# A two-layer decoder trunk on one core: work of layer 1 that waits for room on the vector engine, a later start of the key stage, and a shorter step of the recurrence

## The chip, the core and the metric

The kernel runs on one core of a Trainium2 chip. A core has a matrix engine (TensorE, PE in the profile; its weight loads are PEld), a vector engine (VectorE, DVE), a scalar engine (ScalarE, ACT), a general one (GpSimd, POOL), and SyncE (SP), which here only issues transfers. The program fixes the order of the instructions on each engine (the helper `InOrder`). An instruction whose input is late therefore holds up what is listed behind it on that engine. The metric is the device time of one execution in microseconds (us). The runs of the kernel before took 2396.8, 2400.13 and 2401.81 us, so the median is 2400.13 us.

## What is computed

The input is x with 512 positions of 2048 features. Layer 0 is forgetting attention and layer 1 is RWKV-7 time mixing. Both sit between a modulated RMS norm and a gated residual addition. All of the change lies in layer 1, cut here to what matters:

```
xr, xw, xk, xv, xa, xg = h + (shifted h - h) * mu[i]
r, k, v, z = xr @ Wr, xk @ Wk, xv @ Wv, xg @ Wz          # 2048 x 2048 each
decay, a, mix of v:  low-rank products tanh(xw @ w1) @ w2, (xa @ a1) @ a2, (xv @ v1) @ v2
kk = normalised(k * k_k);  k = k * (1 + (a - 1) * k_a)
S = S * w + (S a) b + v k ;  y = S r                      # a scan over 512 positions, 32 heads
y = group_norm(y) * lnx_w + lnx_b + sum(r * k * r_k) * v  # the last term is the "bonus"
out = x + gate * ((y * silu(z)) @ Wo)
```

## The kernel before, in words

Every large product is computed from float32 operands that are split in two parts each, `hi` and `lo`. ACT writes the `hi` part (a copy with rounding), DVE or POOL subtracts to get the `lo` part, and PE runs three matmuls of 128 x 128 by 128 x 512 for each block of 128 features. Weights arrive in blocks of four such tiles (`raw`, three buffers), and ACT makes `whi` and DVE makes `wlo` from each.

Layer 1 is written as a *backbone* and *tasks*. The backbone is the list of all output tiles of Wk, Wr, Wv, Wz and Wo, 16 tiles for each matrix (some of Wk's are made earlier), each with 16 steps of three matmuls into a PSUM bank named `pj`. The tasks are Python generators. When one says `yield 3`, it is resumed three planner units later. The planner's clock `fl.t` is advanced by every matmul listed, by its columns over 2400, so three matmuls of 512 columns take 0.64 units. After each backbone step, `Flow.run` resumes all tasks that are due, and these list their own instructions. So the planner's clock decides the **order** on every engine, and nothing in it is a real wait on the chip. Real waits are the semaphores that the tiles bring with them.

The tasks are started by `side`, one stage after the other:

- `lora_k`, `lora_w`, `lora_up`: the low-rank products. Their last results go to DRAM (`aad`, `svd`, `ipd`).
- A `yield 3`, then the pools are changed, POOL clears some tiles, and `keys` begins: 16 tasks, one every `KEY` = 9.8 units. A key task loads `ip`, `kt`, `aa`, squares on ACT (`sq`), has the mean of the squares made on PE (helper `means`: ACT `mhi`, DVE `mlo`, two matmuls into bank `S`), and then runs a string of ACT and DVE operations. It stores `at`, `bk`, `gab`.
- `invert` and `inverse`: for each group of four keys, 30 steps of two elementwise operations that invert triangular blocks. Groups 0 to 2 use POOL, group 3 uses DVE (`lt`, `lane`). The results go through `qt`.
- When all of these are done: `stages` and `recur`. `stage` prepares two chunks of 64 positions for a group of eight heads (`rt`, `prk`, `L`, `SV`, `QP`), with 18 transfers of its own. `products` makes their small matrices, `bonus` makes `bv`, and `recur` walks 32 chunks of the recurrence. Each chunk has three dependent links on PE (`x<-SV,L`, `x<-xs,QP`, `x<-SV,tok`), with a DVE copy or sum between them. A link is listed when the planner's clock passes a multiple of `HOP` (3.9 units). `normed` normalises the output of two chunks (`dc`) and stores it to `ypd`.
- `gated` belongs to the backbone tiles of Wz. It takes the silu on ACT (`z`), waits until `ypd` is there, loads it (`yp`, one buffer), and multiplies on DVE. The product goes through `gd` into the activations of Wo.

`mixing` tasks reload the 16 activation tiles when the backbone changes from one matrix to the next. Such a change is a burst of 16 loads `hp`, 16 ACT `hi` and 16 `lo`.

Of the kernel before, what the change touches and what calls it, by code (L numbers as in the profile page):

```python
# [76 lines left out]
class InOrder:  # L77


    def __init__(self, tc, engine):  # L80
        self.tc, self.engine, self.on, self.last, self.clock = tc, engine, False, None, None

    def __getattr__(self, name):
        f = getattr(self.engine, name)

        def issue(*a, **k):
            with ExitStack() as s:
                if self.on and self.last is not None:
                    s.enter_context(self.tc.issue_after(self.last.ins))
                self.last = f(*a, **k)  # L90
            if self.clock and name in ("matmul", "transpose"):
                o, n = a[0], 1
                for d in o.shape[1:]:
                    n *= d
                w = o.shape[0] if a[1].shape[0] > 64 else o.shape[0] * a[1].shape[0] / P
                self.clock.t += (1 if a[2].dtype == R else 4) * n * w / P / 2400
            return self.last
        return issue

    @contextmanager  # L100
    def behind(self):
# [30 lines left out]
def body(ctx, tc, a, out, dbg=None, stop=0):  # L132
    nc = tc.nc
    pe, act, dve, pool, sp = (InOrder(tc, e) for e in (nc.tensor, nc.scalar, nc.vector,
                                                       nc.gpsimd, nc.sync))
# [260 lines left out]
    with ExitStack() as s0:  # L396
# [201 lines left out]
        fl = Flow()  # L598
# [325 lines left out]
        n = len(tiles)  # L924
# [112 lines left out]
    def col(v, j):  # L1037
        return vecs[:, v, j:j + 1]
# [4 lines left out]
    def u3(t):  # L1043
        return t.rearrange("p (u t) -> p u t", u=NU)
# [7 lines left out]
    fl = Flow()  # L1052
# [41 lines left out]
    def read(tag, n):  # L1094
        rings[tag][n] = fl.t + 0.7
# [14 lines left out]
    def take(tag):  # L1110
        while not free[tag]:
            yield 0.2
        free[tag] -= 1
# [363 lines left out]
    def stage(q, g, u):  # L1477

        rt = q.tile([P, NJ, UC, C], F, tag="rt", name="rt", bufs=2)
        sp.dma_start(rt.rearrange("p j c t -> p j (c t)"), rTd[g][:, u])  # L1480
        bk = q.tile([P, NJ, UC, 2, C], F, tag="bk", name="bk", bufs=2)
        yield 1
        for i in range(2):
            for h in range(2):
                sp.dma_start(bk.rearrange("p j c i t -> p (j c) i t")[HS[h], :, i, :],
                             bkd[g][HS[h], u, i ^ h].rearrange("p j (c t) -> p (j c) t", c=UC))
            yield 0.6
        yield from take("prk")
        prk = q.tile([P, NJ, UC, C], F, tag="prk", name="prk", bufs=2)
        sp.dma_start(prk.rearrange("p j c t -> p j (c t)"), ipd[g][:, u])  # L1490
        yield STW
        eI = q.tile([P, NJ, UC, C], F, tag="eI", name="eI", bufs=2)
        act.activation(eI, prk, AF.Exp, scale=-EDEC)
        yield 1
        dec = q.tile([P, NJ, UC], F, tag="dec", name="dec", bufs=3)
        pool.tensor_copy(dec, eI[:, :, :, C - 1])
        dve.tensor_tensor(out=rt, in0=rt, in1=eI, op=OP.mult)
        yield 1
        for j in range(NJ):
            for h in range(2):  # L1500
                s = HS[h]
                dve.scalar_tensor_tensor(out=prk[s, j], in0=rt[s, j],
                                         scalar=vecs[s, V_RK, NJ * g + j:NJ * g + j + 1],
                                         in1=bk[s, j, :, 1 - h, :], op0=OP.mult, op1=OP.mult)
            yield 0.6
        while any(NJ * g + i not in vd for i in range(NJ)):
            yield 0.2
        for c in range(UC):
            yield from take("chunk")
            m = NCH * g + UC * u + c  # L1510
            L, SV = ([q.tile([P, NJ] + w, F, tag=f"{m}{h}", name=f"{m}{h}", bufs=4)
                      for h in range(2)] for m, w in (("L", [2, C]), ("SV", [C])))
            svs[m] = SV
            qp = QP[m % 4]
            for h in range(2):
                s, t = HS[h], OS[h]
                sp.dma_start(L[h][s, :, 0, :], atd[g][s, u, :, c * C:c * C + C])
                dve.tensor_copy(L[h][s, :, 1, :], rt[s, :, c])
                sp.dma_start(qp[h][s], qtd[NJ * g:NJ * g + NJ, 64 * c:64 * c + 64,
                                           4 * h + u, :].rearrange("j p t -> p j t"))  # L1520
                sp.dma_start(SV[h][t], vtd[g][(UC * u + c) * C:(UC * u + c + 1) * C, h])
                if u == c == 0:
                    pool.memset(SV[h][s], 0.0)
                yield 0.6
            fl.start(fl.t + STW, products(q, m, c, L, SV, qp, bk, eI, dec))
            yield 2
        fl.start(fl.t + 2, bonus(q, g, u, prk))
# [41 lines left out]
    def bonus(q, g, u, prk):  # L1569
        vv = q.tile([P, T], F, tag="vv", name="vv", bufs=1)  # L1570
        sp.dma_start(vv.rearrange("p (j t) -> p j t", j=NJ), vvd[g][:, u])
        yield 6
        yield from take("B")
        bo, n = yield from means(q, blkr, prk.rearrange("p j c t -> p (j c t)"), "mh", "ml")
        free["B"] += 1
        yield 0.9
        yield from take("bv")
        bv = q.tile([P, T], F, tag="bv", name="bv", bufs=2)
        dve.scalar_tensor_tensor(out=bv, in0=bo, scalar=float(DH), in1=vv, op0=OP.mult,
                                 op1=OP.mult)  # L1580
        read("S", n)
        free["prk"] += 1
        staged[g, u] = bv

    def hop():
        n = fl.t // HOP
        while fl.t // HOP == n:
            yield 0.1
# [57 lines left out]
    def normed(q, g, u, y):  # L1646

        ys = q.tile([P, T], F, tag="ys", name="ys")
        act.activation(ys, y, AF.Copy)
        while (g, u) not in staged:  # L1650
            yield 0.2
        bv = staged.pop((g, u))
        yield 0.6
        yield from take("B")
        d, n = yield from means(q, centerr, ys, "mh", "ml")
        dc = q.tile([P, T], F, tag="ys", name="dc")
        sq = q.tile([P, T], F, tag="sq", name="sq", bufs=2)
        yield 0.7
        act.activation(sq, d, AF.Square)
        act.activation(dc, d, AF.Copy)  # L1660
        read("S", n)
        yield 1.5
        vr, n = yield from means(q, blkr, sq, "mh", "ml")
        free["B"] += 1
        yield 0.7
        if "silu" in tab:
            tab.clear()
            act.preload_act_table_set("natural_log_exp_and_others")
        r = rstd_of(q, vr, lneps, 64e-5, "sq", False, bufs=2)
        read("S", n)  # L1670
        yield 2
        for j in range(NJ):
            s = slice(j * P, (j + 1) * P)
            dve.scalar_tensor_tensor(out=dc[:, s], in0=dc[:, s], scalar=col(V_LW, NJ * g + j),
                                     in1=r[:, s], op0=OP.mult, op1=OP.mult)
        for j in range(NJ):
            s = slice(j * P, (j + 1) * P)
            dve.scalar_tensor_tensor(out=dc[:, s], in0=dc[:, s], scalar=col(V_LB, NJ * g + j),
                                     in1=bv[:, s], op0=OP.add, op1=OP.add)
        free["bv"] += 1  # L1680
        yield 1.8
        sp.dma_start(ypd[g][:, u], dc.rearrange("p (j t) -> p j t", j=NJ))
        if u == NU - 1:
            yd.update(range(NJ * g, NJ * g + NJ))
# [9 lines left out]
    def gated(j, o, e):  # L1694
        yield from until(e)
        yield from take("z")
        z = mq.tile([P, T], F, tag="z", name="z")
        act.activation(z, o, AF.Silu)
        freed.add(e)
        tab.add("silu")  # L1700
        while j not in yd:
            yield 0.2
        yp = mq.tile([P, T], F, tag="yp", name="yp", bufs=1)
        sp.dma_start(u3(yp), of(ypd, j))
        yield 4
        yield 1
        dve.tensor_tensor(out=z, in0=z, in1=yp, op=OP.mult)
        yield 1
        free["z"] += 1
        if j < KT - 2:  # L1710
            sp.dma_start(gd[j], z)
            zd.add(j)
        else:
            while len(G) < j:
                yield 0.2
            yield from halve(j, z)
# [35 lines left out]

    STW = 5
    DG, DINV = (3,), 32
    HOP = 3.9
    INV, KEY = 54, 9.8

    def side(q):
# [23 lines left out]
                yield 0.8  # L1782
        while len(ups) < 3 * KT:
            yield 0.2
        yield 3
        pools.close()
        kp = pools.enter_context(tc.tile_pool(name="kp", bufs=1, reuse_waits="tile"))
        eIs.append(kp.tile([P, NCH, C + 1], F, name="eI"))
# [40 lines left out]
    tiles += [(a["wo1"][j], G, output, j) for j in range(KT)]  # L1829
    for e in (pe, dve, act):  # L1830
        e.on = True
    pe.clock = fl
    freed.clear()
    n0, n1, n2, n3 = NK, NK + KT, NK + 2 * KT, NK + 3 * KT
    for n, task in ((n0, mixing(1, Ar, A)), (n1, mixing(0, Av, Ar)), (n2, mixing(2, Az, Av)),
# [25 lines left out]
```

## Time and profile before

| | |
|---|---|
| median of three runs | 2400.13 us (2396.8 to 2401.81) |
| profiled execution, its time | 2401.73 us |
| its span, first to last instruction | 2399.9 us |
| PE busy | 2302.2 us (96%) |
| DVE busy | 1605.2 us (67%) |
| ACT busy | 1256.5 us (52%) |
| POOL busy | 694.4 us (29%) |
| mean granted TensorE clock | 0.982 |

The page of the profile gives busy time by engine, then the span in 40 slices (busy tenths; PEclk is the granted TensorE clock in tenths), the chain that ended last, and groups of instructions with their mean time and with what ended the idle time before them. A line of the timeline reads: start, duration, engine, line, operation, output tile `<-` input tiles, sizes, count, and in brackets how long the engine had been idle and what ended that. `SPq` is a transfer being issued.

The first low-rank matmuls of layer 1 stand near 1191 us in the trace. The first loads of the key stage are issued at 1356 us, the recurrence's first links stand at 1738.6 us and its last at about 2172 us, and the product with Wo ends the kernel.

### The profile page before, as it was taken

To read this page: it belongs to the slowest core of one execution; us is meant where nothing else is said; L and a number is where in the kernel's file an instruction comes from. 1 tells how busy PE (TensorE), PEld (TensorE's weight loads), DVE (VectorE), ACT (ScalarE), POOL (GpSimd) and SP (SyncE) were. 2 spreads that over 40 slices of the span, in tenths; PEclk is the share of its full clock that TensorE was granted. 3 is DMA by queue.
4 is the path that set the end of the run, shared out by engine and by line. 5 is a ranking of instruction groups with operands and counts; after the bars stand their busy time and mean duration, and the time that the engine had idled before them with its cause. 6 is when DMAs were issued, how large, how long until landed. Compare 5 with 4: busy or idle time off the path is not lost. (4 is left out here: it accounts for less than half of the span.)

```text
span 2399.9 us, 39413 instructions
## 1 busy us (share of the span) xinstructions
PE 2302.2 (96%) x13626; PEld 1807.3 (75%) x13626; DVE 1605.2 (67%) x2850; ACT 1256.5 (52%) x2300; POOL 694.4 (29%) x1114
## 2 busy tenths in 40 slices
PE   6999999999999999998999898899999899999999
PEld 4787777877778778886777676677777677777787
DVE  6886778888888635336797567666476776755322
ACT  4435655555565545225646777763345556665221
POOL 0002333442424210110141208771245535450000
PEclk8999999999999999999999999899999999999999
DMA  8864466766666346445756999886867766544543
GB/s 307 328 227 156 128 211 217 222 213 213 205 224 220 114 161 225 142 141 157 223 179 198 308 263 277 256 252 187 233 187 195 219 174 194 167 132 154 161 137 97
DMA packets 388152, 480.23 MB, mean 200 GB/s; under 512 B 146032, under 2 KB 217840, under 8 KB 384112
## 3 DMA queue, kind: packets, MB, share of 16 engines
q1 hardware_dynamic: 386288, 475.08, 63.7%
q0 software_dynamic: 1664, 2.63, 0.3%
q8 instruction: 108, 1.77, 0.3%
q14 instruction: 92, 0.75, 0.1%
HBM read 381.63 MB, written 95.95 MB: 199 GB/s over the span
## 5 line engine op out<-in xcount | busy, mean ns | idle before, releaser
L90 PE MATMUL pj<-hi,whi 128*128 128x512 f32 x2416 | 987.4, 409 | 11.0 <-ACT hi L90 8.2
L90 PE MATMUL pj<-hi,wlo 128*128 128x512 f32 x2416 | 959.4, 397 | 10.1 <-DVE wlo L90 10.0
L90 PE MATMUL pj<-lo,whi 128*128 128x512 f32 x2416 | 959.9, 397 | 0.0
L90 DVE TENSOR_TENSOR wlo<-raw,whi 128x512 fp32r<-128x512 f32 (+2 forms) x628 | 473.4, 761 | 255.1 <-ACT whi L90 252.4
L90 ACT ACTIVATE whi<-raw 128x512 fp32r<-128x512 f32 (+2 forms) x628 | 393.9, 634 | 399.0 <-PE pj L90 215.1
L90 PEld LDWEIGHTS pj<-hi,whi 128*128 128x128 f32 x2416 | 459.5, 190 | 116.8 <-ACT hi L90 9.2
L90 PEld LDWEIGHTS pj<-lo,whi 128*128 128x128 f32 x2416 | 458.3, 190 | 108.4 <-DVE lo L90 0.7
L90 PEld LDWEIGHTS pj<-hi,wlo 128*128 128x128 f32 x2416 | 459.9, 190 | 105.2 <-DVE wlo L90 13.4
L90 DVE CUSTOM_DVE_ANT_0 wm<-wm,cb 128x1024 f32<-128x1024 f32 x128 | 155.8, 1217 | 0.3
L90 POOL TENSOR_SCALAR SV<-SV,dec 64x64 f32<-64x64 f32 x224 | 94.2, 442 | 103.9 <-DVE SV L90 69.7
L90 ACT ACTIVATE pr<-Sm,mx 128x128 f32<-128x128 f32 (+3 forms) x128 | 71.5, 559 | 76.8 <-POOL mx L90 76.3
L90 POOL TENSOR_SCALAR pr<-pr,rc 128x128 f32<-128x128 f32 (+3 forms) x128 | 100.8, 788 | 26.0 <-DVE rc L90 23.6
L90 POOL TENSOR_SCALAR mx<-mx 128x1 f32<-128x1 f32 x128 | 59.9, 468 | 143.2 <-DVE mx L90 98.0
L90 DVE CUSTOM_DVE_ANT_0 Sm<-S,cmask 128x128 f32<-128x128 f32 (+3 forms) x128 | 62.3, 487 | 42.5 <-PE S L90 41.8
L90 POOL TENSOR_TENSOR lt<-lane 128x30 f32<-128x30 f32 (+14 forms) x90 | 64.2, 713 | 86.4 <-DMA lane<-mld 79.6
L90 POOL TENSOR_TENSOR bk<-bk,eI 128x512 f32<-128x512 f32 x32 | 36.6, 1142 | 110.3 <-PE S L90 64.0
L90 POOL TENSOR_TENSOR lane<-lane,lt 128x30 f32<-128x30 f32 (+14 forms) x90 | 64.0, 711 | 7.0
L90 PE MATMUL S<-k,q 128*128 128x128 f32 (+7 forms) x256 | 61.9, 323 | 0.0
L90 POOL TENSOR_TENSOR acc<-acc,sq 128x512 f32<-128x512 f32 x14 | 18.1, 1296 | 149.4 <-ACT sq L90 128.2
L90 ACT ACTIVATE pT<-tr 128x512 f32<-128x512 f32 x64 | 31.0, 485 | 54.4 <-PE tr L90 54.4
L90 DVE SCALAR_TENSOR_TENSOR hp<-pj,gate,hp 128x512 f32<-128x512 f32 x16 | 12.0, 751 | 68.0 <-PE pj L90 68.0
L90 PE MATMUL tr<-ident,pr 128*128 128x128 f32 x320 | 56.0, 273 | 1.5 <-DVE pT L90 1.3
(325 smaller groups left out, 3284.0 us busy)
## 6 DMA issues: line engine op xcount, KB each, us to landing
wm<-in_wmodT SPq DMA_DIRECT2D x132, 512.0 KB, 4.4
raw<-in_wz SPq DMA_DIRECT2D x128, 256.0 KB, 3.7
raw<-in_wo SPq DMA_DIRECT2D x128, 256.0 KB, 3.6
raw<-in_wv SPq DMA_DIRECT2D x124, 256.0 KB, 3.9
wm<-in_wmodT SPq DMA_DIRECT2D x30, 1024.0 KB, 6.4
raw<-in_wk SPq DMA_DIRECT2D x96, 256.0 KB, 3.7
raw<-in_wr SPq DMA_DIRECT2D x64, 256.0 KB, 5.0
raw<-in_wq SPq DMA_DIRECT2D x56, 256.0 KB, 3.5
```

Source lines behind the costliest of these rows:

```text
L90: self.last = f(*a, **k)
```

## The change

There are three parts.

First, the helper around each engine gets an estimate of the time until which the engine is taken: `until`, advanced by 0.08 units plus 0.0008 for each column with every instruction listed on it. `dve.room()` makes a task wait, in the planner's clock, until DVE's estimate is no more than 0.6 units ahead. It is called in `stage`, `bonus`, `normed` and `gated`. SP gets the estimate too, but nothing asks for it. Second, the key stage begins 8 units behind the low-rank stage in place of 3. Third, `HOP` is 3.8 in place of 3.9.

```diff
@@ class InOrder
+        self.flow, self.until = None, 0
...
+            if self.flow and "table" not in name:
+                n = 1
+                for d in (k.get("out", a[0] if a else None)).shape[1:]:
+                    n *= d
+                self.until = max(self.until, self.flow.t) + (
+                    0.38 if name == "dma_start" else 0.08 + n * 8e-4)
+    def room(self, left=0.6):
+        while self.until - self.flow.t > left:
+            yield 0.2
@@ stage
+        yield from dve.room()
         dec = q.tile([P, NJ, UC], F, tag="dec", name="dec", bufs=3)
         pool.tensor_copy(dec, eI[:, :, :, C - 1])
         dve.tensor_tensor(out=rt, in0=rt, in1=eI, op=OP.mult)
         yield 1
         for j in range(NJ):
+            yield from dve.room()
             for h in range(2):
                 ...                                  # the two prk of this j
...
             for h in range(2):
                 s, t = HS[h], OS[h]
+                yield from dve.room()
                 sp.dma_start(L[h][s, :, 0, :], atd[g][s, u, :, c * C:c * C + C])
                 dve.tensor_copy(L[h][s, :, 1, :], rt[s, :, c])
@@ bonus
         yield from take("bv")
+        yield from dve.room()
         bv = q.tile([P, T], F, tag="bv", name="bv", bufs=2)
@@ normed
         for j in range(NJ):
+            yield from dve.room()
             ...                                      # dc times the weight and 1/deviation
         for j in range(NJ):
+            yield from dve.room()
             ...                                      # dc plus the bias and bv
@@ gated
-        yield 4
-        yield 1
+        yield 5
+        yield from dve.room()
         dve.tensor_tensor(out=z, in0=z, in1=yp, op=OP.mult)
@@
-    HOP = 3.9
+    HOP = 3.8
@@ side
         while len(ups) < 3 * KT:
             yield 0.2
-        yield 3
+        yield 8
         pools.close()
...
-    pe.clock = fl
+    pe.clock = dve.flow = sp.flow = fl
```

## The prediction

> **What bounds the kernel now.** I read the page first. PE is busy for nearly all of the span, so the time is PE's work plus what PE loses.
>
> ```profile
> span 2399.9 us, 39413 instructions
> PE 2302.2 (96%) x13626; PEld 1807.3 (75%) x13626; DVE 1605.2 (67%) x2850; ACT 1256.5 (52%) x2300; POOL 694.4 (29%) x1114
> PEclk8999999999999999999999999899999999999999
> ```
>
> The change adds and removes no instruction; it reorders them. PE's matmuls stay the same, so it can only move PE's idle time and the time at a lower clock. The second view cuts layer 1 into stretches (length, then busy time of PE, PEld, DVE, ACT, POOL, then granted clock, DMA share, GB/s).
>
> ```profile
> 1302.00:1376.00 74.00, 65.19 (x261) 49.78 (x262) 43.51 (x48) 57.93 (x97) 13.80 (x19) 0.96 0.95 303
> 1376.00:1600.00 224.00, 207.14 (x1412) 159.95 (x1411) 153.11 (x197) 161.07 (x299) 132.08 (x184) 0.94 0.91 262
> 1600.00:1640.00 40.00, 32.91 (x238) 25.12 (x237) 33.39 (x65) 17.44 (x33) 14.46 (x14) 0.87 0.70 219
> 1640.00:2186.00 546.00, 528.96 (x5140) 415.55 (x5141) 361.13 (x766) 293.75 (x516) 222.16 (x427) 0.99 0.66 184
> 2186.00:2240.00 54.00, 51.01 (x216) 39.88 (x215) 27.12 (x48) 26.68 (x44) 0.00 (x0) 1.00 0.60 188
> 2240.00:2400.00 160.00, 156.04 (x672) 126.19 (x670) 45.39 (x68) 33.41 (x53) 0.00 (x0) 1.00 0.42 128
> ```
>
> Length less PE busy is PE's idle time: 8.8 us up to the first key, 16.9 in the keys, 7.1 in the inversion of the last group, 17.0 in the recurrence, 3.0 at its end. The lower clock comes on top: 224 x 0.06 = 13 us in the keys and 40 x 0.13 = 5 in the inversion. So some 53 us of idle time and about 25 of clock lie where the change can reach. The third view is what ended PE's waits, in the inversion (first row), the recurrence (four) and its end (last); columns: total, times, longest.
>
> ```profile
> PE pj L90 <- DVE wlo L90: 7.1, 3, 2.8
> PE S L90 <- ACT GP L90: 9.7, 5, 5.3
> PE S L90 <- ACT mhi L90: 3.5, 1, 3.5
> PE S L90 <- DVE mlo L90: 1.8, 4, 0.6
> PE x L90 <- DVE SV L90: 1.2, 2, 0.9
> PE pj L90 <- DVE wlo L90: 2.9, 3, 1.5
> ```
>
> Last, the chain that ended last, at its end (start, duration, piece).
>
> ```profile
> 2199.92 4.51 DMA yp<-ypd
> 2204.45 0.70 DVE z L90
> ...
> 2226.59 169.46 PE pj L90 x728
> ```
>
> The recurrence's output passes through `yp` and `z` into Wo. PE meanwhile has other tiles and loses only the 2.9 us above. From 2226.59 it runs without a gap: 169.46 / 728 = 0.233 us for each matmul, for which the planner counts 512 / 2400 = 0.213 units. A planner unit is 1.09 us of chip time.
>
> **The change part by part.**
>
> *Keys from 3 to 8 units.* Everything behind this `yield` moves 5 x 1.09 = 5.5 us later against the backbone: POOL's clearing of the tiles, the key loads on SP, all key tasks, the inversions, the start of the recurrence. The place before:
>
> ```profile
> 1355.67 0.58 SPq L90 DMA_DIRECT2D ip<-ipd  x1
> 1365.23 0.63 ACT L90 ACTIVATE hi<-hp 128x512 fp32r<-128x512 f32 x1 [0.89 <-DMA hp<-mxd]
> 1368.94 0.61 ACT L90 ACTIVATE mhi<-sq 128x512 fp32r<-128x512 f32 x1
> 1369.67 0.68 DVE L90 TENSOR_TENSOR wlo<-raw,whi 128x512 fp32r<-128x512 f32 x1
> 1370.28 1.76 DVE L90 TENSOR_TENSOR mlo<-sq,mhi 128x512 fp32r<-128x512 f32 x1
> 1369.61 0.50 PE L90 MATMUL S<-mhi,blkr 128*128 128x512 f32 x1 [3.18 <-ACT mhi L90]
> 1372.09 0.79 PE L90 MATMUL S<-mlo,blkr 128*128 128x512 f32 x1 [1.99 <-DVE mlo L90]
> 1370.00:1375.00 5.00, 3.01 (x8) 2.33 (x8) 4.99 (x5) 4.85 (x9) 2.66 (x2) 0.50 0.96 253
> 1375.00:1380.00 5.00, 5.00 (x20) 4.00 (x19) 3.87 (x6) 3.71 (x8) 0.00 (x0) 0.82 0.97 349
> ```
>
> The first key's `mhi` and `mlo` stand on ACT and DVE among the `hi` and `lo` of the mixing burst that brings Wr's activations, whose loads `hp` are late. PE waits 3.18 + 1.99 = 5.2 us at the key's two matmuls. Then the clock is 0.50 for five us and 0.82 for five, a loss of 2.5 + 0.9 = 3.4, of which 1.0 falls into the 1.99 us idle already counted. Together that is 5.2 + 2.4 = 7.6 us. With the delay PE lists 5.5 us of backbone there, which covers the 5.2. Next late is the backbone's own `wlo`: PE came to the gap at 1369.61 - 3.18 = 1366.4, a block of weights lasts 12 x 0.233 = 2.8 us, so it wants the next at 1369.2, and the `wlo` above ended at 1370.35. I leave 1.5 us for this and its like: **-6** (ends: -7.6, and 0 if another wait takes its place). POOL's clearing and three more loads on SP then stand inside the burst; POOL was busy 13.8 of 74 us there, so I cost them at nothing. If that cover is gone, an odd `lo` is late and it comes out of the 6.
>
> *The other keys.* They move with the first, in the same order to one another: **0**. Ends: -5 (the 5.5 us of lead also shortens later waits), and +6 (rival 1).
>
> *The inversion of the last group* runs on DVE while the next mixing burst puts its `lo` and the `wlo` on the same queue:
>
> ```profile
> 1620.00:1640.00 20.00, 15.67 (x114) 11.90 (x113) 19.39 (x37) 7.06 (x13) 5.22 (x4) 0.82 0.59 163
> ```
>
> DVE is full, and the three waits for `wlo` (7.1 us) are here. The burst belongs to the backbone and stays; the inversion goes 5.5 us later, so 5.5 of some 35 us lie free of it. A share of 5.5 / 35 of 7.1 + 5 is 2; what follows the burst then gets the inversion's end, so I take half: **-1**. Ends: -6, and +5.5 if the end of it delays `wlo` as much as it moves.
>
> Whether short gaps cost clock matters here, since all three are under 3 us. Two stretches of the key stage show it:
>
> ```profile
> 1497.00:1500.00 3.00, 1.49 (x5) 1.00 (x6) 3.00 (x5) 1.63 (x4) 2.74 (x4) 0.95 1.03 322
> 1500.00:1503.00 3.00, 3.00 (x10) 1.89 (x8) 1.73 (x3) 2.19 (x4) 2.63 (x5) 0.50 1.03 316
> ```
>
> After 1.5 us of idle time in three, the next three ran at half clock. [...]
>
> *Hops of 3.8.* 32 chunks of three hops are 96 x 0.1 = 9.6 units, 10.5 us less. Against a start 5.5 us later the recurrence ends 5.0 us earlier beside the backbone. The first and last chunk, and who waits for whom on DVE:
>
> ```profile
> 1738.60 0.91 PE L90 MATMUL x<-SV,L 128*64 128x64 f32 x11
> ...
> 2172.42 0.69 PE L90 MATMUL x<-SV,L 128*64 128x64 f32 x16
> DVE SV L90 <- PE x L90: 47.2, 29, 3.7
> ```
>
> 31 chunks in 433.8 us are 14.0 us each, against 11.7 planned units x 1.09 = 12.8. DVE waits 47.2 us for PE at `SV`, and PE only 1.2 us, in two of 96 links, for DVE. So the links have air, and 0.11 us less in each is hidden there. Ends: +10.5 if each link were tight, +0.2 for the two; I take the latter. The earlier end gives at most the 2.9 us of the last stretch, since PE has no other gap behind the recurrence; as those `wlo` stand behind `z`, and `z` behind `yp`, whose one buffer and 4.5 us per load are unchanged, I take -0.2. Sum **0**, ends -3 and +10.5.
>
> *Room on DVE.* The estimate and the real durations (mean ns after the bar):
>
> ```profile
> L90 DVE TENSOR_TENSOR wlo<-raw,whi 128x512 fp32r<-128x512 f32 x135 | 97.1, 722 | 43.3 <-ACT whi L90 41.7
> L90 DVE SCALAR_TENSOR_TENSOR prk<-rt,vecs,bk 64x128 f32<-64x128 f32 x128 | 47.4, 371 | 1.7
> ```
>
> A 512-column operation counts 0.49 units, 0.53 us, and takes 0.72; a `prk` counts 0.18 units, 0.2 us, and takes 0.37. So DVE looks emptier than it is, and a task is held only where several operations are listed at one instant. Held are `rt`, `prk`, `L`, `bv`, `dc` and `z`; behind each are only its own task's steps, with `QP` and `SV` loads on SP behind the `L` copy, a PSUM bank of `S` behind `bv`, and `ypd` behind `dc`. Stages run up to four chunks ahead and cover a unit or two. In front of them go `wlo`, `mlo` and the links. DVE ended 2.9 + 1.8 + 1.2 = 5.9 us of PE's waits in the recurrence and its end; I take a quarter: **-1.5** (ends: -5.9, and +7, a further stall like the next). The larger waits, 9.7 and 3.5, come through ACT:
>
> ```profile
> 1911.91 0.89 SPq L90 DMA_DIRECT2D prk<-ipd  x1
> 1917.31 0.63 ACT L90 ACTIVATE eI<-prk 128x512 f32<-128x512 f32 x1 [4.09 <-DMA prk<-ipd]
> 1919.39 0.79 PE L90 MATMUL S<-mhi,blkr 128*128 128x512 f32 x1 [5.28 <-ACT GP L90]
> ```
>
> A load `prk` was issued late among another burst's loads, and ACT stood at `eI` with the `GP` that PE needed behind it. No DVE operation is in this, so `room` does not remove it. The stage there moves by +5.5 less 13 chunks x 0.33 = +1.2 us, too little to leave the burst: cost 0.
>
> **Sum.** -6 + 0 - 1 + 0 - 1.5 = -8.5. The profiled execution took 2401.73 us, so 2393.2; the median of the runs is 1.6 us below that execution, so 2391.6 us.
>
> **The rivals.**
>
> 1. *The delay is given back.* The keys stretch has a DMA share of 0.91 and PE waits through it for `mhi` and `mlo`. If the transfers set its pace, a later start of the keys brings a later end, and the 6 us return there as waits. For it: the share. Against it: before the first key the DMA is at 0.95 already, so the delay doesn't idle it. Time: 2391.6 + 6 = 2398.
>
> 2. *Slower: the recurrence does not make up its late start.* A chunk takes 14.0 us now against 12.8 planned, so it may be set by its links and `products` and not by `HOP`, all the more with `L` and `bv` held. Then its end comes 5.5 us later beside the backbone, plus some 3 us for the held `bv` and `dc`, and `yp` and `z`, which already end the chain, hold `wlo` and PE by that much: 8.5 us, and half clock for seven us, 3.5. It decides from where fewer than half of the 9.6 units are gained. Against it: the 47.2 us in which DVE waits for PE. Time: 2391.6 + 12 = 2403.6; with a second stall of 5.3 us like `prk`'s, 2409.
>
> 3. *More than forecast.* The lead carries through the keys (-5), and the inversion leaves the burst (-5 more): 2391.6 - 10 = 2382.
>
> 4. *Room never acts,* since DVE is counted too low: 2393.1, inside the forecast.
>
> **How the numbers follow.** About 0.2% (4.8 us) is what a measurement of this kernel can tell from no change. Forecast with rival 4: 0.45; rival 3: 0.12; rival 1: 0.20; rival 2: 0.23. The first two are faster (0.57), rival 1 is the same (0.20), rival 2 slower in nearly all its range (0.23). The forecast's own range is 2386 to 2396. The whole reaches from 2381, just past rival 3, to 2407, inside the upper end of rival 2; some 0.06 is left out below and 0.12 above.
>
> **What would show it.** First key: PE's wait at `S<-mhi` under 1 us and a clock of 1.0 after it; if it is near 3 again, the first step is wrong. Keys: idle 15 to 18 us over 16 keys; 22 or more is rival 1. Inversion: waits for `wlo` of 5 to 7 us. Recurrence: about 13.7 us per chunk from first to last link; 14.0 is rival 2. PE's waits for DVE in the recurrence fall from 3.0 to about 2, and `ACT GP` stays near 10. The forecast fails if a new wait for a late load stands in front of ACT or DVE somewhere in the new order; one such costs 5 to 9 us.

## The result, and the profile after

The changed kernel takes 2415.79 us (median of five runs, 2413.44 to 2418.25). The kernel before took 2401.81 us in the five runs beside them. The ratio is 1.0058 [1.0043, 1.0072], so the change costs 14.0 us. The forecast was 2391.6 us and faster. It was wrong, in sign and in size.

The page after, its first lines:

```profile
span 2416.5 us, 39388 instructions
PE 2304.7 (95%) x13626; PEld 1806.7 (75%) x13626; DVE 1602.9 (66%) x2850; ACT 1256.0 (52%) x2300; POOL 691.3 (29%) x1114
PEclk8999999999999999999999999989999999999999
```

The work of every engine is what it was. PE has the same 13626 matmuls and 2.5 us more of busy time, so 14.1 of the 16.6 us of span are PE's idle time. The same stretches as in the prediction, cut at the same landmarks (length, then busy time of PE, PEld, DVE, ACT, POOL, then clock, DMA share, GB/s):

```profile
1302.00:1379.00 77.00, 70.53 (x286) 54.08 (x287) 43.61 (x48) 57.97 (x98) 14.68 (x19) 0.98 0.93 303
1379.00:1605.00 226.00, 206.37 (x1408) 158.84 (x1407) 154.20 (x199) 162.54 (x301) 130.33 (x188) 0.95 0.89 257
1605.00:1650.00 45.00, 34.28 (x249) 26.19 (x248) 33.43 (x72) 17.37 (x33) 11.32 (x10) 0.89 0.69 205
1650.00:2200.00 550.00, 525.89 (x5118) 410.26 (x5117) 357.67 (x757) 292.62 (x514) 221.38 (x427) 0.99 0.66 182
2200.00:2260.00 60.00, 53.95 (x222) 43.16 (x221) 28.41 (x49) 26.94 (x45) 0.00 (x0) 0.94 0.58 182
2260.00:2417.00 157.00, 152.68 (x658) 123.43 (x656) 44.11 (x66) 32.24 (x51) 0.00 (x0) 1.00 0.40 124
```

Length less PE busy gives PE's idle time by stage:

| stage | before | after | difference |
|---|---|---|---|
| up to the first key | 8.8 | 6.5 | -2.3 |
| keys | 16.9 | 19.6 | +2.7 |
| inversion of the last group | 7.1 | 10.7 | +3.6 |
| recurrence | 17.0 | 24.1 | +7.1 |
| its end | 3.0 | 6.1 | +3.1 |
| the rest | 4.0 | 4.3 | +0.3 |

That is 14.5 us of idle time (the last stretch after reaches half a us past the end, which is the rest's +0.3). The clock adds nothing over the whole: in the stage at the end it fell from 1.00 to 0.94, 60 x 0.06 = 3.6 us with PE's idle time counted in, but elsewhere it rose, and its mean went from 0.982 to 0.984. Where the 2.5 us of busy time come from is not shown.

**The end.** Before, PE lost 2.9 us there at `wlo`. After, it stands once, at the first matmul of Wo (768 matmuls are left, all 16 tiles of Wo), and then runs at a clock of 0.51. PE's waits, the stretch behind the gap, and the end of the chain:

```profile
PE pj L91 <- ACT z L91: 6.0, 1, 6.0
```

```profile
2230.00:2237.00 7.00, 5.47 (x13) 4.31 (x14) 3.40 (x7) 4.77 (x8) 0.00 (x0) 0.51 0.79 220
```

```profile
2206.58 7.48 PE pj L91 x32
2214.06 0.88 DVE dc L91 x3
2214.96 3.29 DMA ypd<-dc
2218.27 6.68 DMA yp<-ypd
...
2225.70 3.15 DMA yp<-ypd
2229.67 1.21 issue
2231.53 181.16 PE pj L91 x768
```

Read from below: PE needs a PSUM bank that ACT empties into `z`. ACT needs an old `z` that DVE has still to multiply by `yp`. `yp` has one buffer, so the two loads of 6.68 and 3.15 us stand one behind the other, and the first could not start before the recurrence's last `dc` was in `ypd`. In the chain of before the same links end in tiles that PE had other work beside. Here there is none: the 6.05 us and 7 x 0.49 = 3.4 us of clock, of which 0.7 falls into the 1.53 us of that stretch already counted as idle, make about 8.7 us. Since 3.0 us were lost in this stretch before, the end accounts for about 5.7 of the 14.0 us.

**The recurrence.** PE's longest groups of waits there:

```profile
PE S L91 <- ACT GP L91: 6.6, 7, 1.5
PE S L91 <- DVE mlo L91: 6.0, 8, 1.6
PE S L91 <- ACT sq L91: 2.7, 2, 1.4
```

The 5.28 us stall at `ACT GP` of before is gone (its longest is now 1.5), and 4.2 us at `mlo` and many small ones came in its place. With +7.1 us this is the largest row of the table, and no single wait makes it.

**The inversion.** PE's waits, then its one large gap and what DVE did meanwhile:

```profile
PE pj L91 <- DVE wlo L91: 9.9, 4, 6.7
```

```profile
1605.27 0.68 DVE L91 TENSOR_TENSOR wlo<-raw,whi 128x512 fp32r<-128x512 f32 x1
1616.15 0.19 DVE L91 TENSOR_TENSOR lt<-lane 128x30 f32<-128x30 f32 x1 [10.20 <-DMA lane<-mld]
...
1619.11 1.28 DVE L91 TENSOR_TENSOR wlo<-raw,whi 128x512 fp32r<-128x512 f32 x2
1619.84 0.79 PE L91 MATMUL pj<-hi,wlo 128*128 128x512 f32 x1 [6.71 <-DVE wlo L91]
```

DVE stood 10.2 us at the first `lt` of the inversion until the load `lane` had landed, and the `wlo` that PE needed was listed behind it. Before, that wait was there too, but the `wlo` behind it cost PE 2.8 us:

```profile
1605.52 0.19 DVE L90 TENSOR_TENSOR lt<-lane 128x30 f32<-128x30 f32 x1 [10.04 <-DMA lane<-mld]
1610.92 0.50 PE L90 MATMUL pj<-hi,wlo 128*128 128x512 f32 x1 [2.76 <-DVE wlo L90]
```

**The first key.** The two waits of 3.18 and 1.99 us are gone, and another has come. ACT, then PE, then the clock:

```profile
1368.33 0.63 ACT L91 ACTIVATE hi<-hp 128x512 fp32r<-128x512 f32 x1 [1.84 <-DMA hp<-mxd]
1370.30 0.63 ACT L91 ACTIVATE whi<-raw 128x512 fp32r<-128x512 f32 x1 [1.34 <-DMA raw<-in_wr]
1372.20 0.58 ACT L91 ACTIVATE kt<-pj 128x512 f32<-128x512 f32 x1
1372.83 0.50 PE L91 MATMUL pj<-hi,whi 128*128 128x512 f32 x1 [3.25 <-ACT kt L91]
```

```profile
1373.00:1377.00 4.00, 4.00 (x11) 3.19 (x12) 2.10 (x4) 3.08 (x6) 1.14 (x1) 0.57 0.79 242
```

`kt` empties a bank that PE wants for its next tile. It is listed on ACT behind `hi` and `whi`, whose loads are late in the same burst.

### The profile page after: what moved, and what is told of

Read it like the earlier page. It is cut to its first block, busy times and chain, and to the rows that moved or that the text cites. A ratio compares the mean times of both kernels' runs of the same rounds, so it can differ in the third digit from the quotient of the medians.

```text
span 2416.5 us, 39388 instructions
## 1 busy us (share of the span) xinstructions
PE 2304.7 (95%) x13626; PEld 1806.7 (75%) x13626; DVE 1602.9 (66%) x2850; ACT 1256.0 (52%) x2300; POOL 691.3 (29%) x1114
```

## The experiments

Times are medians; the ratio is to the kernel before, run beside them (2399.9, 2400.51, 2400.67 and 2400.27 us in the four sets). Kernels of different sets are compared by their distance to the kernel before of their own set; for the whole change this is 14.0 us. With the 2401.81 us of the result, the medians of the kernel before spread over 1.9 us, so two distances that differ by less than 2 us are not told apart.

**One part alone: the keys.**

```diff
@@ side, ahead of the key pools
-        yield 3
+        yield 8
```

> Only the start of the keys, from 3 to 8 units; no room, hops of 3.9. Theory A (the stage's waits for room hold the recurrence back, and the later start is only made up by the shorter hop): the keys stretch gains about 2 us at the first key as in the changed kernel (3.25 us of wait in place of 5.17), the inversion loses 3 us (a wait of about 6.7 us for wlo behind lt), and the recurrence, 5.5 us later with hops unchanged, ends late and costs 3 to 6 us at Wo: 2403 to 2410, against 2401.8 of before. Theory B (the later keys alone make the loss, through the inversion): 2412 or more, with 14 us or more of extra idle time before 1650 us.

Measured 2419.2 us, 1.0078 [1.0064, 1.0092]. The part that the forecast counted as its gain costs 19 us by itself, more than the whole change, and 9 us above the highest figure of theory A. The time is theory B's, but B's sign is missing: up to 1650 us PE is idle for 75.2 us against 73.8 before, 1.4 more where B asked for 14. The gap ahead of Wo is there (`pj <- ACT z` 5.6 us), with no `room` in the kernel.

**One part alone: the hop.**

```diff
-    HOP = 3.9
+    HOP = 3.8
```

> Only hops of 3.8; keys at 3, no room. Theory A: the recurrence ends some 10 us earlier beside the backbone, links have air, PE has nothing to gain but the last 3 us: 2398 to 2402. Theory C (the shorter hop makes links wait for DVE): 2405 or more, with PE's waits at x for DVE SV and xs together over 4 us, against 1.2 us before.

Measured 2411.89 us, 1.0045 [1.003, 1.0061]. The forecast had 0 for this. PE's waits in the recurrence:

```profile
PE S L90 <- DVE mlo L90: 7.4, 12, 1.5
PE S L90 <- ACT mhi L90: 6.1, 3, 3.9
PE x L90 <- DVE SV L90: 4.6, 7, 1.7
PE S L90 <- DVE vf L90: 3.7, 3, 2.2
```

PE waits for the links' own `SV` 4.6 us in seven links, against 1.2 in two, and 0.6 us for `xs`, so theory C's time and its mark of 4 us are both met. The tight links are few all the same. More is lost at `mlo`, `mhi` and `vf`, which are not links, while the 9.7 us at `ACT GP` of before are 2.0 here. That the denser list of links on DVE makes this other work late is my reading; no run takes it apart.

**One part alone: the rooms.** (`room` in all its places and the estimates, with keys at 3 and `HOP` 3.9.)

> Only the waits for room; keys at 3, hops 3.9. Theory A: stages are held back, idle time in the recurrence rises by 5 us or more over the 16.4 us of before; its end is about as late as before, so Wo's first tiles lose no more than 4 us: 2405 to 2412. Theories B and C: room only reorders, 2398 to 2404.

Measured 2404.35 us, 1.0015 [1.0003, 1.0027]. It lies on the border between what the theories gave: a loss of 4.5 us, where the forecast had a gain of 1.5. Theory A's sign is missing: PE's waits in the recurrence are 15.7 us against 16.5 before. But the execution with the profile, 2399.05 us, is the fastest of twelve, so it doesn't show where the 4.5 us lie.

**Two parts: keys and hop, no room.**

```diff
-    HOP = 3.9
+    HOP = 3.8
@@ side, ahead of the key pools
-        yield 3
+        yield 8
```

> The change without any wait for room: keys at 8, hops 3.8. Theory A: the recurrence makes up its start and ends some 5 us before that of the kernel before; no wait of 6 us at Wo's first tiles; idle time in the recurrence 17 us or less: 2398 to 2406, so at least 10 us less than the changed kernel's 2415.8. Theory B: 2412 or more, since the keys stand as in the changed kernel.

Measured 2415.35 us, 1.0066 [1.0052, 1.0081], the same as the whole change. Theory A was right that no gap would stand ahead of Wo, and wrong about the time, which is B's. PE's loss is inside the recurrence instead: it is idle there for 27.1 us (1638 to 2200 us), against 17.0 before. Singly the three parts cost 19.3 + 12.0 + 4.5 = 36 us; together they cost 14, so they don't add up. The hop, which costs 12 us alone, takes 4 off beside the late keys.

**The changed kernel without the three rooms in `stage`.**

```diff
@@ stage, three times
-        yield from dve.room()
```

> The changed kernel without the three waits for room in the stage (those in bonus, normed and gated stay). Theory A (the stage's waits lengthen the recurrence and bring back its late end): the 6 us wait at Wo's first tiles goes, the time falls by 4 us or more under the changed kernel's 2415.8, to 2406 to 2412. If the stage's waits shield the short hops' links instead: 2415 or more, with PE's waits at x for DVE above 3 us.

Measured 2419.05 us, 1.0081 [1.0068, 1.0094]. Theory A, that held stages bring back the late end and so cost the time, is half borne out: without these rooms the wait ahead of Wo is gone. But A expected the time to fall, and the loss rose from 14.0 to 18.5 us, as the other theory had it. The largest wait that came is one inside a link; PE's waits and the place:

```profile
PE x L91 <- DVE xs L91: 8.3, 2, 7.8
```

```profile
1919.38 0.69 DVE L91 TENSOR_TENSOR wlo<-raw,whi 128x512 fp32r<-128x512 f32 x1 [8.97 <-ACT whi L91]
...
1921.19 0.42 DVE L91 COPY xs<-x 128x256 f32<-128x256 f32 x1
1921.66 0.59 PE L91 MATMUL x<-xs,QP 128*64 128x64 f32 x6 [7.75 <-DVE xs L91]
```

The link's `xs` stood on DVE behind a `wlo` whose `whi` was late. In the changed kernel PE waits only 0.6 us for `xs`; that the held stages move such neighbours apart is read from this one place.

**The changed kernel with the keys back at 3.**

```diff
@@ side, ahead of the key pools
-        yield 8
+        yield 3
```

> The changed kernel with keys at 3 again: room and hops of 3.8 only. Theory D: the recurrence starts at the earlier hop, so the inversion and Wo's first tiles are as before; what is left is the shorter hop's cost in the links, of which room may save some: 2402 to 2411. If keys, hop and room added up: 2411.9 + 4.5 = 2416.

Measured 2401.52 us, 1.0003 [0.9995, 1.0012]. It is just below what the theory of the recurrence's place had given. Rooms and short hops together cost 1.0 us, within the noise; alone they cost 4.5 and 12.0. In the whole change the later keys therefore carry 13.0 of the 14.0 us.

**Late recurrence, with the keys left alone.** A link is listed when the planner's clock passes a multiple of `HOP`:

```
def hop():
    n = fl.t // HOP
    while fl.t // HOP == n:
        yield 0.1
```

A start that moves by a unit therefore moves the recurrence by a whole hop or not at all. This kernel is the one before with the pause ahead of the recurrence's pool one unit longer:

```diff
@@ side, ahead of the pool `rk`
-        yield 3
+        yield 4
```

> Kernel before with one number changed: the recurrence's pool opens 4 instead of 3 units behind the last inversion. Its links are listed on multiples of a hop, so this one unit puts the whole recurrence one hop later, just where the kernel with keys at 8 alone has it; keys and inversions stay as before. Theory D (the loss of keys at 8 comes from the recurrence's place): 2410 to 2418, with a wait of 4 us or more at Wo's first tiles through yp, z and ACT, as in the kernel with keys at 8 alone (2419.2), and the inversion as before (waits for wlo near 7 us). Theory B (it comes from the keys and inversions themselves): within 4 us of before, 2396 to 2404.

Measured 2411.26 us, 1.0047 [1.0033, 1.0061]. One unit on a pause, 1.09 us, costs 11 us, as the theory of the recurrence's place (D) said. The gap ahead of Wo is there (`pj <- ACT z` 6.0 us, longest 5.7). The recurrence and its end, to be set beside the stretches of before from 1640 and from 2186 us:

```profile
1640.00:2192.00 552.00, 530.38 (x5126) 416.48 (x5126) 357.08 (x765) 294.14 (x515) 227.35 (x427) 0.99 0.64 182
2192.00:2252.00 60.00, 53.44 (x228) 41.75 (x228) 27.92 (x48) 27.49 (x45) 0.00 (x0) 0.94 0.55 170
```

At the end PE is idle for 6.6 us against 3.0, and the 12 matmuls behind the gap take 5.3 us (2225.24 to 2230.53), 2.5 more than at 0.233 us each, so some 6 of the 11 us are there. The others are idle time in the recurrence, 21.6 us against 17.0, which the gap ahead of Wo does not explain.

How far the recurrence's end stands from Wo can be counted: the `pj` matmuls from the last `x<-SV,L` to the end (length, PE busy with their count, clock, DMA share, GB/s), before, after, and here:

```profile
2172.90:2425.00 252.10, 217.85 (x927) 1.00 0.41 128
```

```profile
2188.50:2425.00 236.50, 215.80 (x912) 0.98 0.43 134
```

```profile
2184.00:2425.00 241.00, 215.25 (x906) 0.98 0.42 131
```

Wo has 768 of these. From 927 to 906 are 21 matmuls, and one hop of 3.9 units is 3.9 x 2400 / 512 = 18, listed in threes: the recurrence ends a whole hop later beside the backbone. At its first link 1935 are left in place of 1953, which is 18 as well. The kernel with keys at 8 alone has the same two counts.

**Keys earlier.** The kernel before with the keys at 2:

```diff
-        yield 3
+        yield 2
```

> Kernel before with keys at 2 instead of 3: keys 0.64 units earlier, and the recurrence listed in the same hops as before. Theory D: the recurrence stays where it was, so within 4 us of before, 2396 to 2404. Theory F (the order of before is a lucky one, and any shift of the keys costs 8 us or more by new collisions): 2407 or more.

Measured 2407.78 us, 1.0031 [1.0019, 1.0043]. The count stays 927, and there is no gap ahead of Wo. So theory D's range is missed and theory F's time is met. Moving the keys by one step of the backbone, 0.64 units, costs 7 us. One wait of 4.99 us is new, and the one of 5.28 us at `mhi` in the recurrence of before is 7.22 here:

```profile
1638.23 0.28 PE L90 MATMUL x<-t,gab 32*32 32x32 f32 x2 [4.99 <-DVE t L90]
1924.51 0.79 PE L90 MATMUL S<-mhi,blkr 128*128 128x512 f32 x1 [7.22 <-ACT GP L90]
```

So another order alone can cost this much.

**Later keys, the recurrence in its old place.** The kernel before with the keys at 6 and the pause ahead of the recurrence cut by the same 3 units:

```diff
@@ side, ahead of the key pools
-        yield 3
+        yield 6
@@ side, ahead of the pool `rk`
-        yield 3
+        yield 0
```

> Kernel before with keys at 6 units in place of 3, and the pause ahead of the recurrence cut from 3 units to 0, so that the recurrence is listed in the same hops as before. Only keys and inversions stand later, by 3.2 units. Theory D (most of the loss of later keys is that the recurrence starts a hop later and ends too late for Wo): 2400 to 2407, with no wait of 5 us through ACT z at Wo's first tile, against 2419.2 for keys at 8 alone. Theory B (the keys and inversions alone make the loss): 2410 or more.

Measured 2400.72 us, 0.9996 [0.9985, 1.0008]. The count is 927 again. Later keys cost nothing here while the recurrence keeps its place, as theory D said, so it isn't true either that any shift of the keys costs 8 us (F). They gain nothing either: the inversion's gap is 6.4 us in this kernel, and its waits for `wlo` are 9.7 us against 7.1.

**The load `lane`, in the changed kernel.** The first `lt` is listed six units behind the load, and the 30 steps are drawn together by as much:

```diff
@@ invert
         sp.dma_start(m, mld[grp])
+        if grp in DG:
+            yield 6
...
-                yield DINV / 30
+                yield (DINV - 6) / 30
```

> The changed kernel with the first step of the last group's inversion listed 6 units later on DVE (behind the landing of its load of lane), and its steps closer together, so that its end and all behind it keep their place. If the 6.7 us wait for wlo at 1620 us comes from DVE standing at lt until lane has landed: that wait falls under 3 us, and the time by 3 to 6 us under the changed kernel's 2415.8. If DVE's load alone makes it: no change, 2413 to 2418.

Measured 2409.31 us, 1.0037 [1.0023, 1.0051]: 8.6 us above the kernel before, so 5.4 of the 14.0 are gone, within the 3 to 6 expected. DVE's wait, then PE's waits in the inversion and at the end:

```profile
DVE lt L91 <- DMA lane<-mld: 1.2, 1, 1.2
```

```profile
PE pj L91 <- DVE wlo L91: 5.7, 3, 4.2
...
PE pj L91 <- ACT z L91: 6.4, 1, 6.4
```

The wait of 6.71 us behind `lt` is gone; what is left near it is short:

```profile
1618.78 0.50 PE L91 MATMUL pj<-hi,wlo 128*128 128x512 f32 x1 [0.61 <-DVE wlo L91]
```

The 4.2 us are at another `wlo`; the changed kernel's waits for `wlo` behind its large gap are 0.98, 1.00 and 1.23 us. In all the waits for `wlo` fall from 9.9 to 5.7 us. The inversion's part of the loss is shown by this; the end's is untouched.

**The same edit with the keys at 3** (rooms and short hops stay).

> Room and hops of 3.8 with keys at 3 (2401.5 before), and the same later first step of the inversion. The wait of DVE for lane was 10 us there too, but PE lost only some 6 us in the whole inversion: 2397 to 2402, at most 3 us gained.

Measured 2396.68 us, 0.9985 [0.9975, 0.9995]. This is below both kernels, the one before by 4.0 us, and 4.8 us below the same kernel without the edit, where at most 3 were expected. The interval leaves out 1, though the gain is less than the 0.2% of the prediction's bound. Where it comes from is not shown: PE's waits for `wlo` in the inversion are 5.2 us with the edit and 5.3 without, though DVE's wait of 9.4 us for `lane` is gone.

**And the recurrence earlier still.**

```diff
@@ side, ahead of the pool `rk`
-        yield 3
+        yield 1
```

> The same, with the pause ahead of the recurrence cut from 3 units to 1, by which the recurrence ends 7 units earlier beside the backbone. By theory D an earlier end saves the 2 to 3 us still lost at Wo, and with room holding DVE free the short hops cost little: 2393 to 2400, so below both kernels. If a re-ordered recurrence costs new waits as it did with keys at 8 and hops of 3.8 alone: 2403 to 2412.

Measured 2400.26 us, 0.9997 [0.9986, 1.0007]. The count rises from 930 to 966 and the time by 3.6 us. That is at the edge of what theory D gave, and not below both kernels. The end gained what D said: no wait is left there (1.4 us for `z` and 2.4 for `wlo` without this edit). But PE's idle time in the recurrence rose from 16.1 us (1635 to 2180 us) to 21.5 (1634 to 2185), so this order costs more than the earlier end saves.

**The changed kernel with keys at 6 and an early recurrence** (the two edits of the kernel with 2400.72 us, on the changed one).

> Room and hops of 3.8 as in the changed kernel, keys at 6 in place of 8, and the pause ahead of the recurrence cut from 3 units to 0, so that the recurrence starts at the early hop. Theory D (the changed kernel's loss is the recurrence's late place, and the wait for lane in the inversion): the 6 us wait through ACT z at Wo's first tile is gone, the wait for wlo in the inversion stays at 4 to 7 us: 2399 to 2406, 10 us or more under 2415.8. If it takes later keys as such, with room and short hops: 2409 or more.

Measured 2406.27 us, 1.0023 [1.0012, 1.0035], 0.3 us above the range of theory D. The count is 966, the gap ahead of Wo is gone, and the loss is 6.0 us. So 8.0 of the 14.0 went with it, near the 8.7 us that the gap and the clock of 0.51 behind it made. The later keys and the recurrence's place are both altered here, so it is no clean measure of the gap alone.

**The same with the `lane` edit.**

> The same with the first step of the last group's inversion listed 6 units later. Theory D: both causes of the loss are out, 2394 to 2401, level with keys at 3 and the same step (2396.7); then a later start of the keys is worth nothing by itself. If 2392 or less, it is worth something once its costs are taken away; if 2405 or more, a third cause is still there.

Measured 2404.29 us, 1.0017 [1.0005, 1.0029]. That is above what theory D gave and just below its mark for a third cause (2405), so the causes found so far don't account for it. It is 4.0 us above the kernel before of its set, where the kernel with 2400.26 us, which differs in two pauses (keys 3 for 6, and 1 for 0 ahead of `rk`), is 0.4 below its own. Of PE's waits, those for `wlo` in the inversion are larger by 1.4 us (6.2 against 4.8); the rest has no single place. It stays open.

The counts against the time, all kernels:

| kernel | `pj` matmuls left at the first link | at the last | `pj <- ACT z` ahead of Wo, us | us above the kernel before |
|---|---|---|---|---|
| late recurrence alone | 1935 | 906 | 6.0 | 10.8 |
| keys 8 alone | 1935 | 906 | 5.6 | 19.3 |
| the change | 1932 | 912 | 6.0 | 14.0 |
| the change, `lane` later | 1932 | 912 | 6.4 | 8.6 |
| before | 1953 | 927 | none | 0 |
| rooms alone | 1953 | 927 | none | 4.5 |
| keys 2 | 1953 | 927 | none | 7.3 |
| keys 6, recurrence in place | 1953 | 927 | none | 0.1 |
| the change, keys 3 | 1950 | 930 | none | 1.0 |
| that, `lane` later | 1950 | 930 | 1.4 | -4.0 |
| keys 8, hop 3.8 | 1932 | 948 | none | 15.5 |
| the change without `stage`'s rooms | 1932 | 948 | none | 18.5 |
| hop 3.8 alone | 1950 | 966 | none | 12.0 |
| keys 3, `lane` later, recurrence early | 1950 | 966 | none | -0.4 |
| the change, keys 6, recurrence early | 1950 | 966 | none | 6.0 |
| that, `lane` later | 1950 | 966 | none | 4.0 |

All four kernels at 912 or below have the large gap, and none at 927 or above has. The column on the right shows that the gap is not the only cost. The kernels with hops of 3.8 and no rooms in `stage` lose 12 to 18.5 us with no such gap; of the hop alone, the four groups shown are 21.8 us of waits in the recurrence, where the four of before were 16.2. The table also shows what the rooms do. With hops of 3.8 they take the last count from 966 to 930 (keys 3) and from 948 to 912 (keys 8): 36 matmuls, two hops. The first link does not move by this, so the recurrence itself is longer: 1020 matmuls from first to last link, in place of 984. With the pause ahead of `rk` cut to 1 or 0 it is 984 again, rooms and all.

## Why the prediction was wrong, step by step

*Keys from 3 to 8, the first key: -6.* This step failed in part, by the end that it named itself ("0 if another wait takes its place"). The 5.2 us at `mhi` and `mlo` went, and 3.25 us at `kt` with a clock of 0.57 for 4 us came. The stage gained 2.3 us of idle time and about 1.5 of clock (74 x 0.04 before, 77 x 0.02 after), in place of 6. The text looked at what stood behind the key on DVE, found `wlo`, and did not ask what stood behind the burst on ACT.

*The other keys: 0.* 2.7 us were lost, inside the ends. Rival 1 named 22 us or more of idle time as its mark; there are 19.6, above the 15 to 18 of the forecast and below that mark, so it isn't borne out.

*The inversion: -1.* This failed in sign: +3.6 us of idle time. The step saw a queue on DVE that was full, and reckoned with a share of it coming free. But it put all three waits into its full stretch from 1620 us, while the longest, 2.76 us, ended at 1610.92. In the twenty us ahead of that stretch DVE was busy for 33.39 - 19.39 = 14. There the cause was a wait, not work: DVE stood 10 us at `lt` for `lane`, before and after, and what matters is which `wlo` is listed behind that. The prediction shows no row of that wait. The `lane` edit took 5.4 us off the changed kernel's loss.

*Whether short gaps cost clock.* The prediction went by its rows, in which 1.5 us of idle time were followed by three us at a clock of 0.50. Rows of the other kind exist too. The gap of 2.76 us before, and one of 2.75 us in the kernel with the late recurrence, at the same `wlo`, with what followed them; the kernel before first:

```profile
1612.00:1616.00 4.00, 4.00 (x12) 3.15 (x11) 3.93 (x8) 2.08 (x4) 1.46 (x1) 0.57 0.94 347
```

```profile
1611.00:1614.00 3.00, 2.84 (x12) 2.35 (x13) 2.86 (x9) 0.90 (x2) 0.00 (x0) 1.00 0.78 277
1614.00:1617.00 3.00, 3.00 (x14) 2.42 (x14) 2.97 (x4) 2.27 (x5) 2.67 (x2) 1.00 0.77 273
```

The one lost 1.7 us of clock (4 x 0.43), the other none in the six us shown.

*Hops of 3.8: 0.* This was mis-sized. The upper end, +10.5, was tied to tight links. Alone the hop costs 12.0 us, mostly through waits that are not links (`mlo`, `mhi`, `vf`). "The links have air" was right for PE's own wait, and it left out that the links' DVE work is listed among other work. The spacing of the chunks after, first and last `x<-SV,L`, is (2188.5 - 1747.1) / 31 = 14.2 us, not the forecast's 13.7.

*Room: -1.5.* Alone +4.5; with the short hops it takes off 11.0 (12.0 to 1.0). The sign hangs on the rest, and the step had priced it by itself. "Stages run up to four chunks ahead and cover a unit or two" did not hold: two hops of the recurrence are given back. The step also held that the stall of 5.28 us through `prk` would stay; it is gone in the changed kernel.

*Where the recurrence ends.* The sum let the recurrence end 5.0 us earlier beside the backbone. Keys and hop without any room do just that: 948 matmuls left in place of 927, and 21 x 0.233 = 4.9 us. The rooms then take 36 matmuls, 8.4 us, which the room step had put at nothing. So the recurrence ends 15 matmuls, 3.5 us, later than before. This is the step that failed at the end of the kernel, and it is rival 2's mechanism: "`yp` and `z`, which already end the chain, hold `wlo` and PE". Rival 2's condition, that fewer than half of the 9.6 units are gained, is met: from first to last link the shorter hop takes off 6 matmuls (1026 to 1020) in place of 42, which is 1.3 units. The prediction gave rival 2 0.23. It put the lateness at 8.5 us and the clock at 3.5, 12 in all; measured are 3.5 us of lateness, by which PE's idle time there grew from 3.0 to 6.05 us, and 2.7 of clock, 5.7 in all. The argument against it, that DVE waits 47.2 us for PE in the links, speaks of air inside a link and says nothing on the hops over which the rooms spread the work. Rival 2's time, 2403.6 to 2409, was below the 2415.8 since the recurrence's and the inversion's losses came on top.

The rooms alone are not to blame for the forecast's failure. Keys and hop without them end early, have no gap ahead of Wo, and still take 2415.35 us, through waits in the recurrence that the hop's step put at 0.

In all, 8.0 of the 14.0 us went when the recurrence was listed earlier with the keys at 6, 5.4 went with the `lane` edit, and 10.0 with both. The 4.0 that are left are not placed, nor why keys at 8 alone cost 8.5 us more than the late recurrence alone with the same two counts.

## What to carry to other kernels

Where a program fixes the order by a planner's clock in steps, ask of any delay how many whole steps it moves each consumer, and count how much independent work is left between the end of the moved stage and the point that needs it; that count (here 927 or 912) decided whether the matrix engine stood there. It does not give the time: kernels with 948 or 966 left had no such gap and lost up to 18.5 us elsewhere. A queue that looks full can be a queue that stands: look first at the longest wait on each in-order engine, and at what is listed behind it. Parts of a change that each re-order the list don't add up (36 us singly, 14 together), so price them in the order in which they act on each other, or give the sum a wide range on both sides.

## What the runs showed of the hardware

Two gaps of PE of nearly equal length (2.76 and 2.75 us) at the same matmul were followed by four us at a clock of 0.57 in one kernel and by six us at 1.00 in the other. In the changed kernel, gaps of 6.05 and 3.25 us were followed by clocks of 0.51 over 5.5 us and 0.57 over four. With the clock lost behind them, the gaps of 6.05, 3.25 and 2.76 us cost about 8.7, 5.0 and 4.5 us, 1.4 to 1.6 times their length. The one of 2.75 us cost no more than itself, and these rows don't show what made the difference.
